# A two-layer diffusion trunk step on one core: x rebuilt upon an event, modulation sums issued with a margin, the first piece of W1 split into ring slots

## The chip, the cores and the metric

One core of one Trainium2 chip runs the whole program. The metric is the device time of one execution in microseconds, as the median of several; smaller is better. TensorE (PE) multiplies, VectorE (DVE), ScalarE (ACT) and GpSimd (POOL) do the elementwise work, SyncE (SP) issues the DMAs. Every engine works through its own instructions strictly in the order in which they were written out.

## The reference, cut to what matters

640 tokens (128 of context, 512 latent) of 1024 features go through two layers. Each layer has a mixer (layer 0: retention beside differential attention; layer 1: windowed attention beside gated linear attention, GLA) and a squared-ReLU MLP, 1024 to 4096 to 1024. Around both stands the same frame:

```python
mod = (silu(cond) @ w_mod[l] + b_mod[l])        # shift, scale, gate of mixer and of MLP
x = layer_norm(ALPHA * x + gate_a * mixer(x * (1 + scale_a) + shift_a), g_a, b_a)
h = x * (1 + scale_m) + shift_m
x = layer_norm(ALPHA * x + gate_m * (square(relu(h @ w_1)) @ w_2), g_m, b_m)
```

Everything is fp32. The latent tokens have one conditioning vector, the context tokens another.

## The kernel before

**Tiles.** The tokens are NT = 5 tiles of 128. An fp32 product is three float32r products: each operand is split into a high part (`hh`, `whi`, `ghi`) and the rest (`hl`, `wlo`, `glo`), and PE adds high by high, high by low and low by high. In the MLP the hidden features come in 8 groups `g` of 512. For each group, W1 is applied with the weights stationary (matmuls `ff`, 96 per token half), ReLU is squared and split (`relu`, `ghi`, `glo`), and W2 is applied (`fps`, 120 matmuls of 512 columns). In group 0 the first 256 tokens go ahead of the other 384 (`ff1`), since the tiles of the norm ahead become ready one by one; in the trace these are `ff` matmuls of 256 and of 384 columns.

**Weights.** A `Unit` (L507 to L531) is 512 KB of weights. It is loaded into one of three buffers `wraw` and split: ACT copies the high part (`whi`), DVE subtracts (`wlo`), both into rings of NSPL = 5 buffers. `background` (L674) splits ahead of need, by at most five units; while the out projection of the second half holds four, one unit of W1 can be split ahead. A pool of 44 slots of 128x512 fp32, the ring (`slot(...)`), holds nearly everything else, x among it.

**Order.** The program is written out by a planner. It simulates the engines on a clock of its own and decides for each engine which instruction is written next. PE's main work is a list, worked off in order (`order.gemm(step)`). All else are chains: Python generators that are spawned and go on as their turn comes. A chain that yields a number is resumed that many planner microseconds later; one that yields a function, when the function is true; one that yields nothing, when its last instructions are over. On the chip no such wait exists. What the planner leaves is the place of each instruction in its engine's queue, and semaphores for the data alone.

**Modulation.** A `ModChunk` computes 512 columns of `mod` for both conditions in 8 steps (`step`, one per 128 rows of w_mod): POOL multiplies the loaded rows (`wmod`) and adds them up (`moda`), and for the other condition DVE does both in one instruction (layer 1's columns) or ACT and POOL share it (layer 0's). After the eighth step `finish` (L586) issues four small matmuls (`modps`, 256 columns) on PE that add over the partitions. Eight chunks are done in layer 0's mixer, twelve (all of layer 1's) in layer 0's MLP.

**Norm.** `norm` (L859 on) runs once per tile: DVE takes the statistics, POOL writes x <- x * r + nmr in place, PE transposes it (`lnT`), ACT applies scale and shift (`h`) and copies the high part (`hh`), DVE subtracts (`hl`). What the matmuls after it need is complete with `hl`. The residual x still has to be multiplied by the norm's gain and get its bias added: `update` does so on POOL, four instructions of 128x512 per tile (x with `lnrow`), 20 per norm. I call this the rebuild. It is spawned with a delay of UPD = (40, 30) planner microseconds, 40 behind the norm ahead of the MLP (the attention norm), 30 behind the norm after it (the MLP norm). In layer 0 the MLP norm's rebuilt x is written to DRAM and read again by the out projection of layer 1.

**Lines of the profile.** All instructions of DVE, ACT and POOL are recorded at L377, DMAs at L451, matmuls at L467 and transposes at L477; they are told apart by the names of their tiles. In the changed kernel these numbers are one lower, as a constant goes.

Of the kernel before, what the change touches and what calls it, by code (L numbers as in the profile page):

```python
# [9 lines left out]
F32 = mybir.dt.float32  # L10
F32R = mybir.dt.float32r
# [26 lines left out]
LO_POOL = 0  # L38
UPD = (40.0, 30.0)
DRS = False  # L40
# [364 lines left out]
def trunk_kernel(ctx: ExitStack, tc: tile.TileContext, io: dict, layers: int = 2, stop: str = ""):  # L405
# [101 lines left out]
    class Unit:  # L507


        def __init__(self, src, kt, n):  # L510
            self.src, self.kt, self.n = src, kt, n

# [6 lines left out]
        def split(self):  # L519
            tot = self.kt * self.n  # L520
            raw, self.raw = self.raw, None
            hi = wspl.tile([P, UW], F32R, tag="whi", name=nm("whi"))
            lo = wspl.tile([P, UW], F32R, tag="wlo", name=nm("wlo"))
            order.reuse("whi", NSPL, hi)
            order.reuse("wlo", NSPL, lo)
            act.copy(hi[:, :tot], raw[:, :tot])
            vec_tt(lo[:, :tot], raw[:, :tot], hi[:, :tot].bitcast(F32), op=ALU.subtract)
            self.time = order.step[-1]
            self.hi = hi[:, :tot].rearrange("p (k n) -> p k n", k=self.kt)
            self.lo = lo[:, :tot].rearrange("p (k n) -> p k n", k=self.kt)  # L530

    class Piece:


        def __init__(self, units):
            self.units = units
            self.where = [(u, k) for u in units for k in range(u.kt)]

        def hi(self, k, s=slice(None)):
            u, j = self.where[k]  # L540
            return u.hi[:, j, s]

        def lo(self, k, s=slice(None)):
            u, j = self.where[k]
            return u.lo[:, j, s]

    mods, cols = {}, {}

    class ModChunk:
# [36 lines left out]
        def finish(self):  # L586

            l, a = self.l, self.c % 2
            kind = self.c // 2
            if a == 0:  # L590
                mods[l, kind] = dram.tile([2, 2, 512], F32, name=nm("mrow"))
# [37 lines left out]
    for l in range(layers):  # L629
# [8 lines left out]
        for g in range(8):  # L638
            for n in range(2):
                add_piece((l, "1", 2 * g + n), [Unit(io["w_1"][l, 2 * g + n, u], 4, 256) for u in range(2)])  # L640
            for n in range(2):
                add_piece((l, "2", g, n), [Unit(io["w_2"][l, g, n, u], 2, 512) for u in range(2)])
# [31 lines left out]
    def background():  # L674

        saved = order.step
        if pos[0] < min(pos[1] + NSPL, pos[2]) and order.over(units[pos[0]].there):
            split_unit()
# [179 lines left out]

    def norm(t, rows, ft, A, B, final, key, xd=None):  # L859

# [28 lines left out]
        if final:  # L889
# [13 lines left out]
            return  # L903
        def update():
            for a in range(2):
                x = xn[a][:, :512]
# [13 lines left out]
        for a in range(2):  # L920
# [8 lines left out]
            (pool if a < LO_POOL and t < NT - 1 else dve).tensor_tensor(ft.l[a][:, :, tcol(t)], h4, hi.bitcast(F32), op=ALU.subtract)  # L929
        order.spawn(update(), UPD[xd is not None])  # L930
        yield
# [548 lines left out]
    def odd_mixer(ft, cat, out_half):  # L1480
# [343 lines left out]
        value_project((1, "GV0"), ft, G[0].vs)  # L1824
        order.spawn(gla_chain(0))
        sq(0)
        later(lambda: swa(0), 3.5)
# [36 lines left out]
    def layer(l, ft, xd):  # L1864
# [26 lines left out]
        for t in range(NT):  # L1891
            for a in range(2):
                order.gemm(lambda: out_projection(l, cat, env, 1, t, a), cond)
            order.spawn(norm(t, ln, ft, A, B, False, ("m", l, t)))
        del cat, env
# [3 lines left out]
        for g in range(8):  # L1899
            last = g == 7  # L1900
            parts = [(slot("ghi")[:, :TOK].bitcast(F32R), slot("glo")[:, :TOK].bitcast(F32R)) for _ in range(4)]
            if g == 0:
# [47 lines left out]
            else:  # L1950
# [8 lines left out]
                for t in range(NT):  # L1959
                    for nh in range(2):  # L1960
                        order.gemm(lambda: mlp_block(t, nh))
                    order.spawn(norm(t, ln, ft_n, A, B, last_layer, ("h", l, t), xd[t]))
        if last_layer:
# [116 lines left out]
```

## Time and profile before

| | |
|---|---|
| three runs, median | 1718.78 us (1714.31, 1718.78, 1721.03) |
| profiled execution, its own time | 1719.93 us |
| span of that execution in the trace | 1718.1 us |
| PE busy | 1592.2 us, 93% |
| PE weight load (PEld) busy | 1437.5 us, 84% |
| DVE busy | 1096.0 us, 64% |
| POOL busy | 727.4 us, 42% |
| ACT busy | 649.8 us, 38% |
| mean granted TensorE clock | 0.965 |

The span is the time from the first to the last recorded instruction. Layer 0's mixer reaches to about 385 us, its out projection and MLP to about 912 us, layer 1's mixer to about 1170 us and the last MLP to the end. Busy times are unions over an engine's instructions. The granted clock is that of TensorE as the profile's rows show it: 1.00 stands for 2.4 GHz and 0.50 for 1.2 GHz. In a row of the timeline the bracket at the end says how long the engine had been idle before it and whose instruction ended that.

### The profile page before, as it was taken

Reading aid. Unit: us, or ns where it says so; the run is one execution under the profiler, and the core shown is the slowest. Engines: PE = TensorE matmul, PEld = TensorE weight load, DVE = VectorE, ACT = ScalarE, POOL = GpSimd, SP = SyncE. Lnnn points to the kernel's source line nnn. Section 1 sums busy time; section 2 is a strip of 40 time slices with the busy share of each in tenths; the row PEclk is TensorE's granted clock in tenths of the full one; section 3 lists DMA queues with packets and bytes.
Section 4 is the critical chain, followed back from the end, with each engine's and each line's share of the span. In section 5 each row is a group of like instructions: output and inputs, shape, how many; then the busy total and the mean of one; then the engine's idle time right before and its main releaser. Section 6 shows DMA issues by size and latency. Waiting matters only on the chain.

```text
span 1718.1 us, 27804 instructions
## 1 busy us (share of the span) xinstructions
PE 1592.2 (93%) x10869; PEld 1437.5 (84%) x10869; DVE 1096.0 (64%) x1953; ACT 649.8 (38%) x1338; POOL 727.4 (42%) x625
## 2 busy tenths in 40 slices
PE   7888989989888999999899999979989999999995
PEld 4887888889777998898688988869979889988994
DVE  2787875588656666776757678777862444434458
ACT  2564554344431322232126645554443223222221
POOL 1786666671595556555705535431170000000115
PEclk9998999999899999999999999989989999999998
DMA  9432333452245545445232311113212222223221
GB/s 336 155 95 88 108 94 105 126 171 72 69 126 147 142 139 162 137 143 166 86 93 81 114 51 46 30 53 114 75 63 85 74 74 74 74 74 99 74 74 61
DMA packets 89522, 178.22 MB, mean 104 GB/s; under 512 B 23360, under 2 KB 30512, under 8 KB 89392
## 3 DMA queue, kind: packets, MB, share of 16 engines
q1 hardware_dynamic: 89392, 176.46, 32.8%
q8 instruction: 85, 1.39, 0.3%
q14 instruction: 45, 0.37, 0.1%
HBM read 169.92 MB, written 6.50 MB: 103 GB/s over the span
## 4 chain that ended last, share of the span: by engine, by line
PE 70%; DVE 14%; POOL 7%; ACT 4%; issue 3%; DMA 2%; SPq 0%; POOLq 0%; ACTq 0%; DVEq 0%
PE ff L467 24%; PE fps L467 22%; PE proj L467 8%; PE ops L467 4%; POOL moda L377 3%; PE fproj L467 2%; DMA wmod<-in_w_mod 2%; POOL wmod L377 2%; DVE wlo L377 2%; PE early L467 1%; PE po L467 1%; DVE hl L377 1%; POOL x L377 1%; DVE x L377 1%; PE gl L467 1%
## 5 line engine op out<-in xcount | busy, mean ns | idle before, releaser
L467 PE MATMUL ff<-hl,whi 128*128 128x320 f32 (+2 forms) x1024 | 319.8, 312 | 8.8 <-DVE hl L377 8.8
L467 PE MATMUL ff<-hh,whi 128*128 128x320 f32 (+2 forms) x1024 | 321.0, 313 | 4.5 <-ACT hh L377 4.5
L467 PE MATMUL ff<-hh,wlo 128*128 128x320 f32 (+2 forms) x1024 | 319.7, 312 | 3.2 <-DVE wlo L377 3.2
L377 ACT CAST whi<-wraw 128x1024 fp32r<-128x1024 f32 (+1 forms) x187 | 193.8, 1043 | 284.2 <-PE fps L467 220.2
L377 DVE TENSOR_TENSOR wlo<-wraw,whi 128x1024 fp32r<-128x1024 f32 (+1 forms) x187 | 250.3, 1343 | 63.6 <-ACT whi L377 63.3
L467 PE MATMUL fps<-wlo,ghi 128*128 128x512 f32 (+1 forms) x648 | 254.2, 392 | 2.0 <-DVE wlo L377 2.0
L467 PE MATMUL fps<-whi,ghi 128*128 128x512 f32 (+1 forms) x648 | 255.0, 394 | 0.0
L467 PE MATMUL fps<-whi,glo 128*128 128x512 f32 (+1 forms) x648 | 253.9, 392 | 0.0
L377 POOL TENSOR_SCALAR wmod<-wmod,cs 128x512 f32<-128x512 f32 x140 | 141.2, 1009 | 155.3 <-DVE moda L377 132.9
L377 POOL TENSOR_TENSOR moda<-moda,wmod 128x512 f32<-128x512 f32 x140 | 201.6, 1440 | 9.1
L467 PEld LDWEIGHTS ff<-hl,whi 128*128 128x128 f32 x1024 | 195.4, 191 | 10.0 <-DVE hl L377 9.4
L467 PEld LDWEIGHTS ff<-hh,whi 128*128 128x128 f32 x1024 | 195.4, 191 | 8.9 <-ACT hh L377 5.0
L467 PEld LDWEIGHTS ff<-hh,wlo 128*128 128x128 f32 x1024 | 195.3, 191 | 4.0 <-DVE wlo L377 4.0
L377 DVE TENSOR_TENSOR relu<-relu 128x320 f32<-128x320 f32 (+3 forms) x100 | 66.6, 666 | 198.0 <-ACT ghi L377 197.5
L377 POOL TENSOR_TENSOR y<-y,gate 128x512 f32<-128x512 f32 x20 | 33.1, 1659 | 357.2 <-DVE y L377 355.7
L377 ACT ACTIVATE relu<-ff 128x320 f32<-128x320 f32 (+3 forms) x100 | 51.3, 513 | 319.1 <-PE ff L467 319.1
L377 DVE TENSOR_TENSOR y<-fps,y 128x512 f32<-128x512 f32 x120 | 82.5, 689 | 118.1 <-PE fps L467 118.1
L467 PEld LDWEIGHTS fps<-wlo,ghi 128*128 128x128 f32 x648 | 122.0, 188 | 30.2 <-DVE wlo L377 3.3
L467 PEld LDWEIGHTS fps<-whi,ghi 128*128 128x128 f32 x648 | 122.1, 188 | 29.3 <-issue 2.0
L467 PEld LDWEIGHTS fps<-whi,glo 128*128 128x128 f32 x648 | 122.0, 188 | 28.2
L377 POOL TENSOR_TENSOR x<-x,lnrow 128x512 f32<-128x512 f32 (+1 forms) x76 | 113.3, 1510 | 47.0 <-ACT x L377 45.5
L377 POOL TENSOR_TENSOR moda<-moda,modp 128x512 f32<-128x512 f32 x56 | 82.0, 1465 | 88.7 <-ACT modp L377 88.4
(285 smaller groups left out, 3553.9 us busy)
## 6 DMA issues: line engine op xcount, KB each, us to landing
wraw<-in_w SPq DMA_DIRECT2D x128, 512.0 KB
wmod<-in_w_mod SPq DMA_DIRECT2D x192, 256.0 KB
wraw<-in_w_even SPq DMA_DIRECT2D x24, 512.0 KB
wraw<-in_w_out SPq DMA_DIRECT2D x16, 512.0 KB
wraw<-in_w_odd SPq DMA_DIRECT2D x16, 512.0 KB
gate<-mrow SPq DMA_DIRECT2D x16, 256.0 KB
xT<-in_xT SPq DMA_DIRECT2D x8, 320.0 KB
brow<-in_b_mod SPq DMA_DIRECT2D x40, 64.0 KB
```

The source lines that it names most:

```text
L377: i = f(*a, **k)
L467: nc.tensor.matmul(o, a, b, **kw)
```

## The change

It has three parts, in the words of the code:

1. The rebuild no longer starts after a fixed delay. `update` starts with `yield when`: behind the attention norm it waits until group 1 of the MLP begins to be written out, behind layer 0's MLP norm until the projection `sq(0)` of layer 1's mixer does. UPD goes.
2. `finish` starts with `yield 10.0`: the four `modps` matmuls of a chunk are issued 10 planner microseconds later than before.
3. The first piece of W1 of each layer (two units, `own=True`) isn't split into the rings of five but into slots of the 44-slot ring, in pieces of 128x512: per unit two casts on ACT and two subtractions on DVE in place of one each. These units don't count toward the five, so `background` may split them earlier.

```diff
-UPD = (40.0, 30.0)
...
+            if self.own:
+
+                self.hs, self.ls = [], []
+                for k in range(0, self.kt, 2):
+                    c = slice(k * self.n, min(k + 2, self.kt) * self.n)
+                    w = c.stop - c.start
+                    h, l_ = slot("whs")[:, :w].bitcast(F32R), slot("wls")[:, :w].bitcast(F32R)
+                    act.copy(h, raw[:, c])
+                    vec_tt(l_, raw[:, c], h.bitcast(F32), op=ALU.subtract)
...
+            yield 10.0
             if a == 0:
                 mods[l, kind] = dram.tile([2, 2, 512], F32, name=nm("mrow"))
             ps = acc("modps")
...
-                add_piece((l, "1", 2 * g + n), [Unit(io["w_1"][l, 2 * g + n, u], 4, 256) for u in range(2)])
+                add_piece((l, "1", 2 * g + n), [Unit(io["w_1"][l, 2 * g + n, u], 4, 256, g + n == 0) for u in range(2)])
...
-        if pos[0] < min(pos[1] + NSPL, pos[2]) and order.over(units[pos[0]].there):
+        held = sum(not u.own for u in units[pos[1]:pos[0]])
+        if pos[0] < pos[2] and (units[pos[0]].own or held < NSPL) and order.over(units[pos[0]].there):
             split_unit()
...
         def update():
+            yield when
             for a in range(2):
...
-        order.spawn(update(), UPD[xd is not None])
+        order.spawn(update())
...
+        done.add(("SQ", 0))
         sq(0)
...
-            order.spawn(norm(t, ln, ft, A, B, False, ("m", l, t)))
+            order.spawn(norm(t, ln, ft, A, B, False, ("m", l, t), when=lambda: ("g", l, 1) in done))
...
+            if g > 0:
+                done.add(("g", l, g))
...
-                    order.spawn(norm(t, ln, ft_n, A, B, last_layer, ("h", l, t), xd[t]))
+                    order.spawn(norm(t, ln, ft_n, A, B, last_layer, ("h", l, t), xd[t], lambda: ("SQ", 0) in done))
```

Since the planner simulates all engines together, the order of much else shifts as well. The counts hardly do: PE has 9294 rows before and after, ACT 1138 and 1150, DVE 1882 and 1877, POOL 630 and 630.

**POOL at the start of layer 0's MLP.** The first two rows are the last tile's x of the attention norm; rows with `lnrow` are the rebuild; `wmod` and `moda` are the first chunk of layer 1's modulation (`cs` holds the conditions). Before:

```order
L377 TENSOR_SCALAR x_4425<-x_4425,r_5180,nmr_5186 128x512
L377 TENSOR_SCALAR x_4630<-x_4630,r_5180,nmr_5186 128x512
L377 TENSOR_TENSOR x_4259<-x_4259,lnrow_4660 128x512
L377 TENSOR_TENSOR x_4259<-x_4259,lnrow_4664 128x512
L377 TENSOR_TENSOR x_4465<-x_4465,lnrow_4662 128x512
L377 TENSOR_TENSOR x_4465<-x_4465,lnrow_4666 128x512
L377 TENSOR_TENSOR x_4313<-x_4313,lnrow_4660 128x512
L377 TENSOR_TENSOR x_4313<-x_4313,lnrow_4664 128x512
L377 TENSOR_SCALAR moda_5475<-wmod_4455,cs 128x512
L377 TENSOR_SCALAR wmod_4548<-wmod_4548,cs 128x512
L377 TENSOR_TENSOR x_4499<-x_4499,lnrow_4662 128x512
L377 TENSOR_TENSOR moda_5475<-moda_5475,wmod_4548 128x512
```

Now, with five further pairs of `wmod` and `moda` left out between the two pieces:

```order
L376 TENSOR_SCALAR x_4425<-x_4425,r_5166,nmr_5172 128x512
L376 TENSOR_SCALAR x_4617<-x_4617,r_5166,nmr_5172 128x512
L376 TENSOR_SCALAR moda_5489<-wmod_4455,cs 128x512
L376 TENSOR_SCALAR wmod_4499<-wmod_4499,cs 128x512
L376 TENSOR_TENSOR moda_5489<-moda_5489,wmod_4499 128x512
...
L376 TENSOR_SCALAR wmod_5588<-wmod_5588,cs 128x512
L376 TENSOR_TENSOR moda_5489<-moda_5489,wmod_5588 128x512
L376 TENSOR_SCALAR moda_5693<-wmod_5627,cs 128x512
L376 TENSOR_TENSOR x_4134<-x_4134,lnrow_4647 128x512
L376 TENSOR_TENSOR x_4313<-x_4313,lnrow_4647 128x512
L376 TENSOR_TENSOR x_4134<-x_4134,lnrow_4651 128x512
```

The whole first chunk now stands ahead of the rebuild, and all 20 instructions of the rebuild stand within the second chunk (`moda_5693`). Before, six stood ahead of the first chunk and 14 within it. In layer 1's MLP there is no modulation, and POOL's order there is what it was: ten x with r and nmr, then the 20 of the rebuild.

**PE at the second chunk's sums.** `hh`, `hl`, `whi`, `wlo` belong to W1 of group 1, `ghi`, `glo` with `fps` to W2. Before, the four matmuls stand in group 1 of layer 0's MLP, 24 `ff` matmuls ahead of the end of its W1:

```order
L467 MATMUL ff_5970<-hl_4677,whi_5760 128x320
L467 MATMUL ff_5970<-hh_4675,wlo_5761 128x320
L467 MATMUL modps_6000<-moda_5688,ones 32x256
L467 MATMUL modps_6000<-moda_5689,ones 32x256
L467 MATMUL modps_6000<-moda_5688,ones 32x256
L467 MATMUL modps_6000<-moda_5689,ones 32x256
L467 MATMUL ff_6018<-hh_4674,whi_5659 128x320
```

Now they stand behind 108 of the 120 `fps` of the same group:

```order
L466 MATMUL fps_6215<-whi_6060,ghi_5716 128x512
L466 MATMUL fps_6215<-wlo_6061,ghi_5716 128x512
L466 MATMUL fps_6215<-whi_6060,glo_5717 128x512
L466 MATMUL modps_6229<-moda_5692,ones 32x256
L466 MATMUL modps_6229<-moda_5693,ones 32x256
L466 MATMUL modps_6229<-moda_5692,ones 32x256
L466 MATMUL modps_6229<-moda_5693,ones 32x256
L466 MATMUL fps_6244<-whi_5967,ghi_5710 128x512
```

That is 132 matmuls later (24 `ff`, 108 `fps`). The first chunk's sums stand 24 `ff` later than before, the twelfth's 108 matmuls later.

**POOL from layer 0 to layer 1.** Around the rebuild stand the first instructions of GLA's first head group: `gA` is set to zero, `Eq` and `Ek` are computed level by level (128x5x64 is the first level). Before, the last rows of the rebuild and what follows:

```order
L377 TENSOR_TENSOR x_4598<-x_4598,lnrow_9152 128x512
L377 MEMSET gA_10013 128x5
L377 MEMSET gA_10021 128x5
L377 TENSOR_TENSOR x_4598<-x_4598,lnrow_9156 128x512
L377 TENSOR_TENSOR x_4425<-x_4425,lnrow_9150 128x512
L377 TENSOR_TENSOR x_4425<-x_4425,lnrow_9154 128x512
L377 TENSOR_TENSOR x_4630<-x_4630,lnrow_9152 128x512
L377 TENSOR_TENSOR x_4630<-x_4630,lnrow_9156 128x512
L377 TENSOR_TENSOR Eq_10184<-gA_10021 128x5x64
L377 TENSOR_TENSOR Eq_10184<-gA_10013 128x5x64
L377 TENSOR_TENSOR Ek_10185<-gA_10013 128x5x64
```

Now, from the last x with r and nmr on, with seven rows of the rebuild left out:

```order
L376 TENSOR_SCALAR x_4617<-x_4617,r_9584,nmr_9590 128x512
L376 MEMSET gA_10001 128x5
L376 MEMSET gA_10009 128x5
L376 TENSOR_TENSOR x_4134<-x_4134,lnrow_9158 128x512
...
L376 TENSOR_TENSOR x_4425<-x_4425,lnrow_9158 128x512
L376 TENSOR_TENSOR Eq_10172<-gA_10009 128x5x64
L376 TENSOR_TENSOR x_4425<-x_4425,lnrow_9162 128x512
L376 TENSOR_TENSOR Eq_10172<-gA_10001 128x5x64
L376 TENSOR_TENSOR Ek_10173<-gA_10001 128x5x64
L376 TENSOR_TENSOR Ek_10173<-gA_10009 128x5x64
L376 TENSOR_TENSOR x_4465<-x_4465,lnrow_9160 128x512
```

Nine rows of the rebuild stay ahead of GLA's first level; one stands within it and ten between it and the second level.

On DVE, between the attention norm's last `nmr` and its last `hl`, that one counted, stood 9 instructions in either layer; now 14 do. The changed order has three `wlo` there in place of one, as W1's second piece can be split there too.

In both mixers the last transposes of the heads' outputs (`catT`), which the out projection of the second half h=1 needs, have moved within the 240 `ops` matmuls of the first half h=0: in layer 0 from behind 192 of them to behind all 240, in layer 1 from behind 96 to behind 216.

## Rows read from the trace of the kernel before

**Rows 1.** The page: span, and each engine's busy time with its share.

```profile
span 1718.1 us, 27804 instructions
...
PE 1592.2 (93%) x10869; PEld 1437.5 (84%) x10869; DVE 1096.0 (64%) x1953; ACT 649.8 (38%) x1338; POOL 727.4 (42%) x625
```

**Rows 2.** Windows (columns in the first line): layer 0's mixer, layer 1's mixer, last MLP.

```profile
core 0: us, PE busy (x) PEld busy (x) DVE busy (x) ACT busy (x) POOL busy (x), PEclk, DMA share, GB/s
70.00:385.00 315.00, 280.11 (x2179) 263.27 (x2177) 232.62 (x531) 160.44 (x387) 215.41 (x174) 0.95 0.37 111
...
912.00:1170.00 258.00, 238.92 (x2376) 215.42 (x2376) 193.74 (x457) 143.01 (x372) 121.75 (x134) 0.96 0.20 65
...
1278.00:1670.00 392.00, 392.00 (x2183) 354.39 (x2182) 165.40 (x212) 108.02 (x151) 17.43 (x11) 1.00 0.25 81
```

**Rows 3.** PE's waits: us in total, times, longest.

```profile
PE modps L467 <- POOL moda L377: 13.1, 4, 4.6
PE ff L467 <- DVE hl L377: 8.8, 2, 4.5
...
PE ff L467 <- ACT hh L377: 4.5, 2, 2.2
...
PE modps L467 <- DVE moda L377: 3.6, 2, 2.1
...
PE ff L467 <- DVE wlo L377: 3.2, 4, 1.0
```

**Rows 4.** Timeline of PE, layer 0's MLP: start us, us, instruction, [idle before <-releaser].

```profile
499.53 0.71 PE L467 MATMUL modps<-moda,ones 128*32 128x256 f32 x6 [4.64 <-POOL moda L377]
...
525.36 1.08 PE L467 MATMUL modps<-moda,ones 128*32 128x256 f32 x6 [3.86 <-POOL moda L377]
...
851.30 1.08 PE L467 MATMUL modps<-moda,ones 128*32 128x256 f32 x6 [4.32 <-POOL moda L377]
```

**Rows 5.** Windows as in rows 2: what follows three of these waits, and `ff`'s wait for `hl` in layer 0.

```profile
499.94:503.36 3.42, 3.42 (x16) 3.19 (x13) 0.45 (x2) 0.00 (x0) 3.42 (x5) 0.50 0.85 281
525.36:530.67 5.31, 5.31 (x22) 4.50 (x23) 1.98 (x4) 0.00 (x0) 2.58 (x3) 0.50 0.46 121
...
851.30:854.93 3.63, 3.63 (x12) 2.34 (x13) 2.44 (x4) 0.00 (x0) 2.42 (x2) 0.50 0.13 52
...
440.10:445.33 5.23, 5.23 (x16) 5.23 (x17) 0.54 (x1) 0.00 (x0) 1.02 (x1) 0.50 0.00 0
```

**Rows 6.** Timeline of DVE: start of layer 0's MLP.

```profile
425.50 0.42 DVE L377 TENSOR_TENSOR relu<-relu 128x256 f32<-128x256 f32 x1
...
431.08 1.40 DVE L377 TENSOR_TENSOR relu<-relu 128x256 f32<-128x256 f32 x1
```

**Rows 7.** Timeline of POOL: layer 0's MLP, its end, layer 1's MLP.

```profile
429.95 9.54 POOL L377 TENSOR_TENSOR x<-x,lnrow 128x512 f32<-128x512 f32 x6
...
461.45 0.94 POOL L377 TENSOR_SCALAR wmod<-wmod,cs 128x512 f32<-128x512 f32 x1 [20.33 <-DVE moda L377]
...
928.93 23.36 POOL L377 TENSOR_TENSOR x<-x,lnrow 128x512 f32<-128x512 f32 x15
...
1248.69 30.18 POOL L377 TENSOR_TENSOR x<-x,lnrow 128x512 f32<-128x512 f32 x20
```

**Rows 8.** The page's costliest groups (line, engine, instruction, count | busy us, mean ns | idle before).

```profile
L377 POOL TENSOR_SCALAR wmod<-wmod,cs 128x512 f32<-128x512 f32 x140 | 141.2, 1009 | 155.3 <-DVE moda L377 132.9
L377 POOL TENSOR_TENSOR moda<-moda,wmod 128x512 f32<-128x512 f32 x140 | 201.6, 1440 | 9.1
```

**Rows 9.** Chain that ended last, layer 1's out projection and last MLP: start us, us, what.

```profile
1186.86 19.97 PE ops L467 x168
...
1278.38 28.02 PE fps L467 x120
1306.40 28.16 PE ff L467 x192
```

**Rows 10.** Timeline of DVE behind layer 1's last transposes.

```profile
1188.81 1.55 DVE L377 TENSOR_TENSOR catl<-soT,cath 128x640 fp32r<-128x640 f32 x2
```

More of the change, by code (lines that the diff above doesn't have):

```diff
@@ L507, in trunk_kernel, with __init__ @@
     class Unit:
-        def __init__(self, src, kt, n):
-            self.src, self.kt, self.n = src, kt, n
+        def __init__(self, src, kt, n, own=False):
+            self.src, self.kt, self.n, self.own = src, kt, n, own
         def load(self):
@@ L521, in split @@
             raw, self.raw = self.raw, None
+            if self.own:
[6 more added lines that the diff above has]
+                    vec_tt(l_, raw[:, c], h.bitcast(F32), op=ALU.subtract)
+                    self.hs.append(h)
+                    self.ls.append(l_)
+                self.time = order.step[-1]
+                return
             hi = wspl.tile([P, UW], F32R, tag="whi", name=nm("whi"))
@@ L537, in __init__, with part @@
             self.where = [(u, k) for u in units for k in range(u.kt)]
+        @staticmethod
+        def part(u, tiles, j, s):
+            return tiles[j // 2].rearrange("p (k n) -> p k n", n=u.n)[:, j % 2, s]
         def hi(self, k, s=slice(None)):
             u, j = self.where[k]
-            return u.hi[:, j, s]
+            return self.part(u, u.hs, j, s) if u.own else u.hi[:, j, s]
         def lo(self, k, s=slice(None)):
             u, j = self.where[k]
-            return u.lo[:, j, s]
+            return self.part(u, u.ls, j, s) if u.own else u.lo[:, j, s]
     mods, cols = {}, {}
@@ L857, in summed, with norm @@
             stt(x, x, ALPHA, y, op0=ALU.mult, op1=ALU.add)
-    def norm(t, rows, ft, A, B, final, key, xd=None):
+    def norm(t, rows, ft, A, B, final, key, xd=None, when=None):
         cuts = [(0, 0, 512), (1, 0, 512)] if t < NT - 1 else [(0, 0, 256), (0, 256, 512), (1, 0, 256), (1, 256, 512)]
```

## The prediction

> **What bounds the kernel now.** I read the page first: PE is busy for 93% of the span [rows 1], and a span of 1718.1 less 1592.2 us of work leaves 126 us in which it does nothing. So a change that adds or takes no matmul can win only out of these 126 us, or out of stretches in which PE works at a lower clock. Next, the windows, to see where the 126 us lie. The last MLP has none of them: 392.00 busy of 392.00 us at a granted clock of 1.00 [rows 2]. Layer 0's mixer has 34.9 (315.00 less 280.11), layer 1's 19.1 (258.00 less 238.92) [rows 2]. Then the list of PE's waits, for what the change can reach: the sums `modps` wait 13.1 us for POOL's `moda` and 3.6 for DVE's; at the starts of the two MLPs `ff` waits 8.8 us for `hl`, 4.5 for `hh`, 3.2 for `wlo` [rows 3]. That is 33 us in all. Last, windows behind such waits: the granted clock stands at 0.50 for some us, though PE has work without a gap [rows 5]. A wait costs more than its own length here.
>
> **Modulation sums with a margin.** This removes waits and adds none by itself. All of DVE's 3.6 us and 12.8 of POOL's 13.1 (4.64, 3.86 and 4.32, the three long ones [rows 4]) fall on the first, second and twelfth chunk in layer 0's MLP, where PE otherwise has no cause to stop: 16.4 us. Behind the three waits PE works 3.42, 5.31 and 3.63 us at 0.50 [rows 5]; at 1.00 these take half, so 6.2 us more are at stake. Together 22.6 us. Do the sums now come late enough? An `ff` matmul takes 28.16 / 192 = 0.147 us and an `fps` 28.02 / 120 = 0.233 [rows 9].
>
> - First chunk: the sums move by 24 `ff`, 3.5 us. That is less than the wait of 4.64, but POOL's chain for the chunk loses 14 instructions of the rebuild. A rebuild's instruction takes 30.18 / 20 = 1.51 us [rows 7], so it loses 21 us and ends long before.
> - Second chunk: the sums move by 24 `ff` and 108 `fps`, 3.5 + 25.2 = 28.7 us. But the whole rebuild, 30.2 us, now stands inside this chunk's chain, with seven times `wmod` and `moda` at 1.009 + 1.440 [rows 8], 17.1 us, so the chain is 47.3 us long. It begins when the first chunk's ends. If that chunk's `wmod` is released at 461.45 as before [rows 7], the first chunk ends near 479 and the second near 526. PE gets there near 525.36 − 3.86 − 1.4 − 4.64 − 1.7 − 6 + 28.7 = 536 (its old time, less the two waits ahead of these sums, the earlier wait with its slow stretch and the next paragraph's gain, plus the shift). The margin is 10 us; it is the smallest.
> - Twelfth chunk: 108 matmuls later, at least 15.9 us, against waits of 4.32 and 2.1.
>
> I take −22. Ends: −14 if the second chunk's sums still wait by half of what they did and the clock falls once more, −23 if all goes. The `modps` themselves and the DMA of their result move along; the next reader of layer 1's columns is its own mixer, hundreds of us later.
>
> **Rebuild behind layer 0's attention norm.** Six instructions of it run at 429.95, for 9.54 us [rows 7], just while DVE prepares the last operands of the MLP. A `relu` of 256 columns takes 0.42 us at 425.50 and 1.40 at 431.08 [rows 6]: beside the rebuild each DVE instruction takes about 1 us longer. Of the waits at MLP starts, 16.5 us in two layers [rows 3], layer 0 has 8.1: one of each of the two pairs for `hh` and `hl` (2.2 and 4.3) and half of the four for `wlo`. The 5.23 us of work at 0.50 behind the last one [rows 5] cost another 2.6. Of these 10.7 us I expect 6 back. With the rebuild moved behind the first chunk DVE works at the short durations; but 14 instead of 9 instructions now stand ahead of the last `hl`, and ACT's part of the chain (`h`, `hh`), which POOL does not slow, then ends last. Ends: −3.5 (only the two `hl` and `wlo` parts shrink), −8.5.
>
> **Rebuild behind layer 1's attention norm.** By the order nothing moves: the planner's event has no other POOL work to let pass, so the 20 instructions follow the last `nmr` as before and run for 30.18 us from 1248.69 [rows 7]. DVE goes on being slowed there, and has five more instructions. At 1.40 us each [rows 6] these would put `hl` 7 us later, but they start some 3 us earlier, as the `wlo` in front of them have gone into ring slots earlier, and 1 us of wait for `wlo` goes. I take 0, between −3 and +5.
>
> Here a rule stands against the change. Rows 6 show DVE slowed to about the pace of one of POOL's instructions, 1.40 against 1.51 us, not stopped for longer. The Trainium skill, in "SBUF — State Buffer", section "SBUF: two separate sides", says that the port pair of VectorE and GpSimd is an exclusive lock, which an instruction holds until its end, while the other fully blocks. The rows agree for the small `relu`. By that rule each of the five added instructions could wait for a whole one of POOL's, 5 × 1.51 = 7.6 us, and with no earlier start the sum would be some 7 us higher; that is a rival below.
>
> **Rebuild from layer 0 to layer 1.** Fifteen of its instructions ran from 928.93 for 23.36 us [rows 7] beside the last `hl`. Nine still do; the other eleven, 17 us, now stand in and behind the first GLA level. For DVE at this place: 0. The x that goes through DRAM lands later by about 20 us, which the out projection, more than 100 us on, doesn't notice. For GLA see the next part.
>
> **The mixers' order.** That is the cost that the trace of before doesn't show. The last transposes now come behind 240 instead of 192 of layer 0's h=0 matmuls, and 216 instead of 96 in layer 1. What stands between them and h=1 covers the way from transpose to `catl`: 19.97 / 168 = 0.119 us per matmul [rows 9], so 5.7 us of cover become none, and 17.1 become 2.9. The way itself is a copy, a cast and the subtraction, of which two take 1.55 us [rows 10]; I put it at 3 to 5 us. So +2.5 to 3 in layer 0 and +2 to 2.5 in layer 1. In return, later transposes may wait less for the heads. Sum: +5; ends −8 (a quarter of the mixers' 54 us of idle time goes, less the cover lost) and +18 (GLA in layer 1 late by most of 17 us and half of layer 0's way in front).
>
> **Split of the own units.** Four casts and four subtractions of 512 columns in place of two and two of 1024: the same columns, on engines that are far from full, earlier than the stretch that matters. 0.
>
> Sum: −22 − 6 + 0 + 0 + 5 + 0 = −23 against 1719.93 us, the profiled execution's own time: 1697. The median of the runs shown is 1718.78, 1.1 lower; I leave the sum as it is.
>
> **Rivals.**
>
> - *Sums that still wait.* The second chunk has a margin of 10 us out of estimates; if DMA or DVE hold up the first chunk, the rebuild's 30 us in the chain eat it. For it: POOL's wait of 20.33 us for DVE ahead of the first chunk [rows 7]. Against it: all other chunks have no rebuild any more. Price: half of the 22 and the 6 kept back, so about 1707 us.
> - *The mixers gain as well.* The planner fitted all of it anew; were 20% to 30% of the 54 us idle in mixers to go, about 1683. Against it: nothing in the change aims there.
> - *The mixers eat the savings.* The covers of 5.7 and 17.1 us are lost, and heads end no earlier: +17 more, about 1714, within the noise.
> - *Slower: GLA's chain gets too late.* Eleven instructions of the rebuild, 17 us, stand on POOL ahead of the second level's `Eq` and `Ek`. If POOL, not PE, sets the pace of the levels, the last transposes of layer 1 come 17 us later, without the 14 us of cover, and the half clock behind such a wait adds some 5. 1719.93 − 28 for the two gains + 36 for this is 1728, and 1733 with the start of layer 1's MLP 5 us worse. It decides once these losses exceed the gains by the measurement's bound, some 37 us in all. Against it: POOL is 42% busy [rows 1] and 122 of 258 us in this mixer [rows 2], so it can catch up.
> - *Each added DVE instruction in layer 1 waits for a whole one of the rebuild*, 5 × 1.51 us, and none starts earlier: about 1704. For it: 1.40 against 0.42 us [rows 6]. Against it: the added `wlo` find their operands ready earlier.
>
> **How the numbers follow.** Forecast (1688 to 1706) 0.43; added DVE instructions blocked 0.05; sums that still wait 0.19; mixers gain 0.10; mixers eat it 0.14; slower 0.09. I predict 1697 us. The range is 1681 to 1716: it leaves out the slower rival and the edges. A measurement can tell about 0.5% from no change here, 8.6 us. Forecast, blocked DVE, waiting sums and mixers' gain are faster by more than that, 0.77, of which I take off 0.02 as 1707 lies close to the bound: faster 0.75, same 0.16, slower 0.09.
>
> **What would show it.** In the profile of the changed kernel: no `modps` row with a bracket above 1 us in layer 0's MLP, and no window at 0.50 behind one; PE busy nearly all of 500 to 850. At the start of layer 0's MLP the `relu` at 0.4 and not 1.4 us and the wait for `hl` at 2 us or less; in layer 1 still 20 x with `lnrow` in one run beside a `hl` wait of about 4.5 us. Ahead of h=1, new waits for `catl` of 2 to 3 us in both layers. The prediction is wrong if the waits for `moda` stay, or if the mixers (70 to 385 and 912 to 1170) get longer by more than 10 us together.

## The result, and the profile after

The changed kernel takes 1705.82 us, the median of 8 runs (1699.45 to 1711.06), against 1717.43 us before (8 runs, 1714.31 to 1721.03). The ratio is 0.9933, with a 95% interval of 0.9917 to 0.9949: faster by 0.67%, or 11.6 us. The forecast was 1697, with a range of 1681 to 1716. The profiled execution took 1705.05 us with a span of 1702.9, so it stands 15.2 us under the span of before [rows 1], 3.6 us more than the medians differ by.

I cut both spans at the same places of the program: the first `ff` and the first `fps` of each layer, and layer 1's first `proj`. Windows of the kernel before; columns as in rows 2. From top to bottom: layer 0's mixer with the out projection, the start of its MLP, the rest of its MLP, layer 1's mixer with the out projection, the start of its MLP, the rest.

```profile
0.10:417.40 417.30, 364.67 (x2819) 333.49 (x2819) 288.03 (x645) 193.94 (x457) 249.53 (x213) 0.94 0.43 136
417.40:459.30 41.90, 33.78 (x211) 32.73 (x210) 26.42 (x48) 22.09 (x50) 14.75 (x11) 0.88 0.16 51
459.30:916.40 457.10, 439.68 (x2438) 386.79 (x2436) 307.44 (x366) 127.59 (x191) 259.74 (x209) 0.98 0.44 131
916.40:1236.10 319.70, 299.50 (x2885) 273.82 (x2883) 240.32 (x560) 166.75 (x423) 131.26 (x142) 0.97 0.23 72
1236.10:1278.20 42.10, 33.77 (x211) 32.87 (x210) 31.08 (x48) 22.11 (x50) 32.71 (x24) 0.88 0.15 50
1278.20:1718.10 439.90, 420.78 (x2317) 377.83 (x2316) 202.66 (x290) 117.33 (x167) 39.38 (x27) 0.98 0.24 78
```

The same six windows of the changed kernel:

```profile
0.10:416.30 416.20, 362.56 (x2818) 332.30 (x2819) 289.61 (x653) 193.82 (x459) 249.33 (x213) 0.95 0.43 139
416.30:450.50 34.20, 31.50 (x212) 30.14 (x211) 20.13 (x44) 22.07 (x52) 6.55 (x5) 1.00 0.19 63
450.50:887.10 436.60, 432.31 (x2438) 381.75 (x2436) 309.27 (x366) 126.66 (x190) 280.06 (x215) 1.00 0.44 134
887.10:1223.10 336.00, 303.49 (x2885) 277.04 (x2884) 244.06 (x567) 167.10 (x426) 130.95 (x142) 0.95 0.23 72
1223.10:1263.50 40.40, 33.42 (x212) 32.00 (x211) 35.11 (x44) 22.01 (x52) 36.09 (x24) 0.92 0.17 53
1263.50:1702.90 439.40, 420.24 (x2317) 377.80 (x2315) 199.81 (x288) 116.41 (x166) 39.53 (x27) 0.98 0.23 76
```

The first number behind the window is its length. The six differences are −1.1, −7.7, −20.5, **+16.3**, −1.7 and −0.5 us. They add up to −15.2. So the change won 31 us and lost 16, and the loss sits in one place: layer 1's mixer. There PE is idle for 32.5 us in place of 20.2, and its work takes 303.5 in place of 299.5 us, since more of it runs at the lower clock (mean 0.95 in place of 0.97).

PE's waits in the changed kernel (us in total, times, longest), the lines that answer to rows 3 and the new ones of some size:

```profile
PE ff L466 <- DVE hl L376: 6.8, 6, 4.6
...
PE sqT L476 <- DVE ropea L376: 6.4, 2, 5.9
...
PE ops L466 <- DVE tmp L376: 4.0, 1, 4.0
PE ops L466 <- ACT pT L376: 4.0, 1, 4.0
...
PE fps L466 <- DVE glo L376: 3.3, 1, 3.3
```

The sums' 16.7 us in rows 3 are gone; no `modps` stands in the list any more. `ff` still waits once for 4.6 us for `hl`, now in layer 1 alone. New are the wait of the query transposes `sqT` for `ropea` (the rotary embedding of the windowed attention's queries), two waits of `ops` in the mixers, and one of `fps` for `glo`.

How the second chunk's sums went. POOL's timeline of the changed kernel: the first `wmod` that had to wait for DVE, the end of the first chunk, the rebuild inside the second chunk, and the end of this chunk:

```profile
452.65 0.93 POOL L376 TENSOR_SCALAR wmod<-wmod,cs 128x512 f32<-128x512 f32 x1 [25.45 <-DVE moda L376]
...
472.65 1.30 POOL L376 TENSOR_TENSOR moda<-moda,wmod 128x512 f32<-128x512 f32 x1
...
474.59 15.17 POOL L376 TENSOR_TENSOR x<-x,lnrow 128x512 f32<-128x512 f32 x9
...
493.47 15.42 POOL L376 TENSOR_TENSOR x<-x,lnrow 128x512 f32<-128x512 f32 x9
...
525.46 1.30 POOL L376 TENSOR_TENSOR moda<-moda,wmod 128x512 f32<-128x512 f32 x1
```

And PE's, at the sums that need it:

```profile
535.85 0.64 PE L466 MATMUL modps<-moda,ones 128*32 128x256 f32 x8
```

POOL ends at 526.8 us and PE comes at 535.9: a margin of 9 us, where the prediction had 526 and 536. There is no bracket on PE's row, so it waited for nothing. That POOL's end came out to the microsecond is partly luck: its chain was released at 452.65, 8.8 us before the 461.45 that the prediction took over from before, but the first chunk took 21.3 us in place of 17.5 and the second 52.8 in place of 47.3.

### The profile page after: what moved, and what is told of

Its sections match the earlier page's. It is cut to its first block, busy times and chain, and to the rows that moved or that the text cites. A ratio compares the mean times of both kernels' runs of the same rounds, so it can differ in the third digit from the quotient of the medians.

```text
span 1702.9 us, 27816 instructions
## 1 busy us (share of the span) xinstructions
PE 1583.5 (93%) x10869; PEld 1431.0 (84%) x10869; DVE 1098.0 (64%) x1957; ACT 648.1 (38%) x1342; POOL 742.5 (44%) x625
## 5 line engine op out<-in xcount | busy, mean ns | idle before, releaser
L466 PE MATMUL ff<-hh,whi 128*128 128x320 f32 (+2 forms) x960 | 297.0, 309 | 0.0
L466 PE MATMUL ff<-hh,wlo 128*128 128x320 f32 (+2 forms) x960 | 296.2, 308 | 0.0
L466 PE MATMUL ff<-hl,whi 128*128 128x320 f32 (+2 forms) x960 | 296.1, 308 | 0.0
L376 DVE TENSOR_TENSOR wlo<-wraw,whi 128x1024 fp32r<-128x1024 f32 (+1 forms) x183 | 245.8, 1348 | 76.3 <-ACT whi L376 76.1
L376 ACT CAST whi<-wraw 128x1024 fp32r<-128x1024 f32 (+1 forms) x183 | 189.4, 1045 | 251.7 <-PE fps L466 230.3
L376 POOL TENSOR_TENSOR moda<-moda,wmod 128x512 f32<-128x512 f32 x140 | 206.9, 1478 | 9.4
L376 DVE TENSOR_TENSOR relu<-relu 128x320 f32<-128x320 f32 (+3 forms) x100 | 74.3, 743 | 179.6 <-ACT ghi L376 178.7
L466 PEld LDWEIGHTS ff<-hh,whi 128*128 128x128 f32 x960 | 180.2, 188 | 3.4 <-issue 2.5
L466 PEld LDWEIGHTS ff<-hl,whi 128*128 128x128 f32 x960 | 180.2, 188 | 0.6
L466 PEld LDWEIGHTS ff<-hh,wlo 128*128 128x128 f32 x960 | 180.2, 188 | 0.0
```

Source lines behind the costliest of these rows:

```text
L376: i = f(*a, **k)
L466: nc.tensor.matmul(o, a, b, **kw)
```

## The experiments

Line numbers in the excerpts are those of the profile of each kernel; they differ by one or two. "Middle" is the third window above, "start" the second or the fifth, "mixer" the fourth.

**1. The later sums alone** (the kernel before with one line more).

```diff
             kind = self.c // 2
+            yield 10.0
```

> The kernel before with one line of the change alone: the modulation sums issued 10 planner microseconds later. If the sums' waits are what the middle of layer 0's MLP gained (457.1 us from its first W2 matmul to layer 1's first projection before, 436.6 after), this stretch alone falls to 437 +-2 us here too, with no modps wait above 1 us. Layer 1's mixer stays at about 320 us if the rebuild's event made it 336 long; the total would then be some 19 to 23 us under the kernel before, about 1696, and so under the changed kernel. Rival: any shift of the planner's order costs layer 1's mixer some 16 us, whatever caused it; then the total is 1700 to 1705 and this mixer takes about 335 us.

Measured: 1701.64 us, ratio 0.9919 (0.9900 to 0.9937). The mixer takes 319.3 us, as in the theory, and the middle 443.0, not 437. No `modps` waits, but `fps` now waits 6.55 us for `glo` in group 1. The rival has the total (1700 to 1705) and not its cause, as the mixer didn't grow to 335. So this one line is worth as much as the whole change, and it doesn't cost the mixer anything.

**2. The events alone**, without the later sums and without the slots.

```diff
-            yield 10.0
...
-[Unit(io["w_1"][l, 2 * g + n, u], 4, 256, g + n == 0) for u in range(2)]
+[Unit(io["w_1"][l, 2 * g + n, u], 4, 256 ) for u in range(2)]
```

> The rebuild upon an event alone, without the later sums and without W1's split into slots. If the event makes layer 1's mixer longer, it takes about 336 us here (320 before), layer 0's MLP start takes about 36 to 38 us in place of 41.9, and the middle of layer 0's MLP stays near 455 or loses some of its waits, since the chunk's chain on POOL is free of the rebuild for the first chunk: total 1722 to 1732, slower than before. Rival, that the mixer's loss comes from the other two parts: mixer at 320, total 1708 to 1714.

Measured: 1730.07 us, ratio 1.0079 (1.0064 to 1.0094), slower than before. Mixer 339.5, first start 36.6, middle 454.6: as the theory had it. In the middle the waits of the sums are replaced by one of 9.65 us of `fps` for ACT's `ghi`; run 10 shows where that comes from.

**3. The changed kernel with a narrow rebuild behind layer 0's MLP norm.** The planner sees the full instructions, the chip gets 16 of 512 columns, so x is rebuilt there only in part; every engine's order is the same.

```diff
-                pool.tensor_tensor(x, x, rows[0][a][:, :512], op=ALU.mult)
+                pool.tensor_tensor(x, x, rows[0][a][:, :512], op=ALU.mult, narrow=16 if key[0] == "h" else 0)
```

> The changed kernel with every engine's order as it is, but the 20 instructions of the rebuild behind layer 0's MLP norm are 16 columns wide in place of 512, so x is rebuilt there only in part: the rest keeps its place, and POOL no longer reads and writes beside DVE from 943 to 957 us. Theory: the contention of the moved rebuild with DVE makes the 5.89 us wait of the transposes of the windowed attention's queries for ropea and the 13.65 us at half clock behind it; then the wait is under 2 us, the clock does not fall there, and layer 1's mixer takes 321 to 326 us in place of 336: total 1693 to 1696. Rival: the new place of ropea on DVE, behind the first GLA level, makes the wait; then it stays above 4 us, the mixer at 332 to 336, and the total at 1702 to 1706.

Measured: 1703.91 us (0.9925, 0.9906 to 0.9944), mixer 336.3. The theory falls. PE's wait and DVE's row ahead of it in the changed kernel:

```profile
968.48 0.66 PE L476 MATMUL sqT<-cst,qq 128*128 128x128 f32 x2 [5.89 <-DVE ropea L376]
```

```profile
962.23 2.00 DVE L376 COPY gST<-gl 64x320 f32<-64x320 f32 x4 [1.41 <-PE gl L466]
```

Timelines of this run's kernel, PE first:

```profile
965.63 0.66 PE L478 MATMUL sqT<-cst,qq 128*128 128x128 f32 x2 [5.89 <-DVE ropea L378]
```

```profile
953.08 0.82 DVE L378 TENSOR_TENSOR Ek<-Ek,gkT 128x640 f32<-128x640 f32 x1
959.38 2.00 DVE L378 COPY gST<-gl 64x320 f32<-64x320 f32 x4 [5.48 <-PE gl L468]
961.39 3.27 DVE L378 TENSOR_TENSOR_SCAN gA<-ones,ge 128x128 f32<-128x128 f32 x10
964.67 0.82 DVE L378 TENSOR_TENSOR ropea<-proj,cst 128x256 f32<-128x256 f32 x3
```

The wait is 5.89 us, to the hundredth the same as in the changed kernel, though DVE was early here: it stood idle for 5.48 us, in place of 1.41, waiting for PE's `gl` (the scores of the first GLA level). Behind that wait, on DVE's queue, stand the copy of `gl`, ten scans and then `ropea`, 2.00 + 3.27 + 0.82 us. PE's queue has `sqT` right behind `gl`. So PE runs `gl` and then waits for the whole row behind it, however fast anyone was before. Two queues that fit together badly make this wait, not contention.

**4. The changed kernel with a narrow rebuild behind layer 1's attention norm**, likewise (`narrow=16 if key[:2] == ("m", 1) else 0`), so x is rebuilt only in part there.

> The changed kernel with every engine's order as it is, but the 20 instructions of the rebuild behind layer 1's attention norm are 16 columns wide, so x is rebuilt there only in part. Theory: the 4.59 us wait of ff for hl and the half clock behind it (6.83 us) come from the rebuild that runs beside DVE; then the wait falls below 1.5 us, the clock stays at 1.00, and the time from the first ff to the first W2 matmul falls from 40.4 to 34 us, as in layer 0 (34.2): total 6 us less than the changed kernel, about 1700. Rival: the 14 instructions ahead of the last hl are too many for DVE in any case; then it stays at 39 to 40 and the total at 1705.

Measured: 1696.26 us (0.9886, 0.9862 to 0.9910). The window of layer 1's MLP start:

```profile
1218.30:1252.40 34.10, 31.45 (x210) 30.14 (x209) 20.09 (x43) 21.92 (x52) 12.80 (x24) 1.00 0.20 62
```

34.1 us at a clock of 1.00, against 40.4 at 0.92. What is left of layer 1's wait for `hl` is the rebuild beside DVE, and nothing else.

**5. The event behind layer 0's MLP norm taken back**, the old delay of 30 put in its place; all else as in the changed kernel.

```diff
-            yield when
+            yield when if xd is None else 30.0
```

> The changed kernel, with the rebuild behind layer 0's MLP norm put back to its delay of 30 planner microseconds; the event behind the attention norm, the later sums and the slots stay. Theory: that one event moves the first GLA level 72 matmuls later on PE, right ahead of the transposes of all five tiles' queries, and this order costs layer 1's mixer its 16 us. Then the mixer falls from 336 to 318 to 324 us with all else as in the changed kernel, and the total is about 1690. Rival: the sums' 10 us or the slots shift the mixer's order just as much: mixer 330 or more, total 1700 or more.

Measured: 1690.86 us (0.9846, 0.9823 to 0.9869), mixer 322.1 us. The window of the mixer:

```profile
885.60:1207.70 322.10, 297.10 (x2886) 271.83 (x2884) 244.77 (x567) 167.16 (x425) 133.27 (x142) 0.97 0.23 75
```

The theory stands for the event: taking it out of the changed kernel gives the mixer 14 us back. PE's order in this kernel has its transposes of the queries spread among the projections again.

**6. The event set one projection later**, ahead of `sq(1)`.

```diff
-        done.add(("SQ", 0))
         sq(0)
...
+        done.add(("SQ", 0))
         sq(1)
```

> The changed kernel with the event of the rebuild behind layer 0's MLP norm set one projection later: ahead of sq(1) in place of sq(0). The first GLA level then stands on PE where it stood before the change. Theory (the late first level is what costs): mixer 318 to 325 us, total 1688 to 1695. Rival (a rebuild anywhere inside the mixer costs, for DVE or for the planner): mixer 330 to 340 us, total 1700 to 1708, with new waits behind sq(1).

Measured: 1715.59 us (0.9991, 0.9979 to 1.0002), mixer 350.1. The theory that only the late first level costs falls: this order has the first level in its old place and loses 14 us more, beyond the rival's 340 too. POOL, ACT and PE in this kernel:

```profile
1029.24 12.06 POOL L376 TENSOR_TENSOR x<-x,lnrow 128x512 f32<-128x512 f32 x9
1041.26 1.25 POOL L376 TENSOR_TENSOR gqb<-gA 128x640 f32<-128x640 f32 x1
```

```profile
1042.55 0.74 ACT L376 ACTIVATE gqb<-gqb 128x640 f32<-128x640 f32 x1 [16.13 <-POOL gqb L376]
...
1050.49 0.74 ACT L376 ACTIVATE Eq<-Eq 128x640 f32<-128x640 f32 x1 [4.04 <-POOL Eq L376]
1051.13 0.58 ACT L376 COPY sqT<-sqT 128x128 f32<-128x128 f32 x3
```

```profile
1051.43 1.12 PE L476 MATMUL spT<-cst,sp 128*128 128x128 f32 x4 [15.05 <-ACT sqT L376]
```

Nine instructions of the rebuild stand ahead of `gqb` on POOL. ACT waits 16.13 us for `gqb` and, further on, 4.04 us for `Eq`, both from POOL; copies of `sqT`, which need nothing from POOL, are queued behind both; PE waits 15.05 us, until one of these copies is done at 1051.4.

**7. The same with a narrow rebuild behind the MLP norm**, every engine's order as in run 6, x again rebuilt only in part there.

> The kernel with the event at sq(1), every engine's order as it is, but the 20 instructions of the rebuild behind layer 0's MLP norm 16 columns wide, so x is rebuilt there only in part. Theory: nine of them, 12 us, stand on POOL ahead of gqb; ACT waits for gqb 16.13 us with a copy of sqT queued behind it, and PE waits 15.05 us for that. Then that wait falls to 3 us or less, the stretch at half clock around it goes, and layer 1's mixer falls from 350 to 322 to 332 us; total 1688 to 1698. Rival: as in the changed kernel, the order alone costs, and narrow instructions change nothing: mixer 345 to 350, total 1712 to 1716.

Measured: 1699.43 us (0.9891, 0.9875 to 0.9908), mixer 333.6; the same wait on PE and ACT's wait now:

```profile
1041.76 1.11 PE L478 MATMUL spT<-cst,sp 128*128 128x128 f32 x4 [6.21 <-ACT sqT L378]
```

```profile
1033.91 0.74 ACT L378 ACTIVATE gqb<-gqb 128x640 f32<-128x640 f32 x1 [3.50 <-POOL gqb L378]
```

Both readings were half right. Of the 30 us that this mixer loses against before, 16.5 are the rebuild's time on POOL and some 14 are order that stays bad when the rebuild costs nothing.

**8. The rebuild waits on the chip.** Run 5, and ahead of the first tile's rebuild POOL reads one column of the last `hl`.

```diff
+            if key[0] == "m" and t == 0:
+                pool.tensor_scalar(sm("seen", [P, 1]), ft.l[1][:, 0, TOK - 1:TOK].bitcast(F32), cs[:, 0, 0:1], 0.0, op0=ALU.mult, op1=ALU.add)
```

> As the run with the old delay, and one instruction more per attention norm: POOL reads one column of the last hl ahead of the first tile's rebuild, so that the rebuild waits on the chip, not only in the planner, for DVE's last operand of the MLP. Theory: in layer 1 nothing else held the rebuild back from DVE; with the wait the time from the first ff to the first W2 matmul falls from 40 to about 34 to 35 us, with no wait for hl above 1.5 us and no half clock there; total 6 us under the run with the old delay, about 1684. Rival: the rebuild then slows DVE in the rest of group 0 and PE waits for glo in place of hl: the same 40 us and no gain in total.

Measured: **1684.62 us, ratio 0.9814 (0.9793 to 0.9835)**, the shortest median here. POOL in layer 1:

```profile
1233.07 0.30 POOL L376 TENSOR_SCALAR seen<-hl,cs 128x1 f32<-128x1 f32 x1 [9.83 <-DVE hl L376]
1233.33 29.84 POOL L376 TENSOR_TENSOR x<-x,lnrow 128x512 f32<-128x512 f32 x20
```

The start of layer 1's MLP takes 34.2 us. The 30 us of rebuild run beside the `ff` matmuls of the later half, and PE doesn't wait for `glo` in layer 1, so the rival falls.

**9. Later sums and slots, no event.**

```diff
-            yield when
...
-        order.spawn(update())
+        order.spawn(update(), UPD[xd is not None])
```

> The later sums and W1's first piece in slots, without either event. Against the run with the later sums alone (1701.6 us) this shows what the slots bring by themselves. Theory: little; the start of layer 0's MLP stays at 41 us as the rebuild still runs beside the last hl, only the two waits for wlo (0.97 and 0.6 us) may go, mixers as in that run: total 1699 to 1703. Rival: the slots, not the event, shortened the start of layer 0's MLP: 34 to 37 us there, total 1693 to 1697.

Measured: 1697.87 us (0.9886, 0.9867 to 0.9906). The starts take 37.6 and 40.3 us (41.2 and 42.1 in run 1), the middle 443.9, the mixer 319.7. The theory is off: the slots alone shorten both starts, by 3.6 and 1.8 us. The rival has the first start nearly right and the total not.

**10. Run 8 without the slots.**

```diff
-[Unit(io["w_1"][l, 2 * g + n, u], 4, 256, g + n == 0) for u in range(2)]
+[Unit(io["w_1"][l, 2 * g + n, u], 4, 256 ) for u in range(2)]
```

> The kernel whose rebuild waits on the chip for the last hl (1684.6 us), without the slots for W1's first piece. If the slots bring something by themselves (1701.6 against 1697.9 us in the two runs without the events), the starts of the two MLPs take 35 to 37 us in place of 34.1, with waits for wlo of 1 and 0.6 us and for hh of 2.2 us again: total 1687 to 1691. Rival: with the rebuild gone from DVE they bring nothing: starts at 34, total 1684 to 1686.

Measured: 1702.54 us (0.9915, 0.9900 to 0.9929). Both starts take 36.8 us, as expected, some 2.7 more each. But the total is 18 us over run 8, half of it in the middle (448.6 against 439.2). ACT and PE there:

```profile
508.33 1.05 ACT L376 CAST whi<-wraw 128x1024 fp32r<-128x1024 f32 x1 [0.70 <-PE ff L466]
527.56 0.72 ACT L376 ACTIVATE moda<-wmod,cs 128x512 f32<-128x512 f32 x1 [18.18 <-DMA wmod<-in_w_mod]
528.19 0.42 ACT L376 ACTIVATE relu<-ff 128x320 f32<-128x320 f32 x1
528.64 0.47 ACT L376 ACTIVATE ghi<-relu 128x320 fp32r<-128x320 f32 x1
```

```profile
529.16 0.79 PE L466 MATMUL fps<-whi,ghi 128*128 128x512 f32 x1 [10.89 <-ACT ghi L376]
```

ACT's first instruction of a modulation chunk waits 18.18 us for its rows of w_mod, with `relu` and `ghi` of the MLP queued behind it. Run 2 has the same on ACT, with 16.63 us. But the late load is not what sets run 10 apart from run 8, where ACT waits about as long for it:

```profile
508.16 0.47 ACT L376 ACTIVATE ghi<-relu 128x320 fp32r<-128x320 f32 x1
...
526.44 0.73 ACT L376 ACTIVATE moda<-wmod,cs 128x512 f32<-128x512 f32 x1 [15.93 <-DMA wmod<-in_w_mod]
```

There `relu` and `ghi` stand ahead of the waiting instruction, in run 10 behind it: the order decides. That the load is late because the rebuild holds POOL, and with it the buffers of w_mod, fits all three runs; it was not tried by itself.

**11 and 12. Run 8 with the event at group 2, and (likewise, with a 4) at group 4.**

```diff
-when=lambda: ("g", l, 1) in done
+when=lambda: ("g", l, 2) in done
```

> The kernel whose rebuild waits on the chip for the last hl, with its event one group later, at group 2 of the MLP. Theory: the 3.3 us wait of fps for glo in group 1 of layer 0 (and 6.8 us at half clock behind it) comes from the rebuild beside DVE in that group; in a later group PE meets it with more ahead, or it moves along to group 2. If it goes: middle of layer 0's MLP 433 us in place of 439, total 1679; if it moves along, 437 to 440 and 1684.

> The same with the event at group 4. Expected as for group 2: 1679 if the wait for glo belongs to group 1 alone, 1684 if the rebuild slows DVE before an fps in any group; x must be ready for group 6 (ALPHA x enters there), which leaves two groups, some 110 us, for 30 us of work, so no loss from that.

Measured: 1687.95 us (0.9834, 0.9814 to 0.9854) and 1696.22 us (0.9877, 0.9862 to 0.9892). The wait of `fps` for `glo` moves along with the rebuild and grows: 3.31 us in group 1, 4.59 in group 2, 8.62 and 3.20 in group 4. Both totals are above the two that were expected (1679 or 1684). Group 4 is worse than group 1; groups 1 and 2 are not told apart, as the intervals overlap. Why the wait grows was not looked into.

## Why the prediction was right, and where it was not

The time lies in the range, and most terms came near their size; the term for the mixers did not. The prediction called itself wrong if the two mixers together got longer by more than 10 us. With their out projections they got longer by 15.2, so by its own sign its account of the mixers is wrong. That the time still fell just inside the 1688 to 1706 of the forecast's case is luck. It is close to the 1707 of the rival whose sums still wait, but those waits didn't come; the loss is of the size of the rival whose mixers eat the savings (+17), from another cause.

**Modulation sums: right for the whole change, not for the later sums alone.** Expected −22, measured −20.5 in the middle. The waits and the half clock behind them went. But the later sums by themselves bring 14.2 there (run 1), and the event behind the attention norm another 5.7 (443.9 in run 9, 438.3 in run 5, which differ in this event alone). What is missing is the new wait of 3.3 us for `glo` in group 1, which the prediction didn't have: there the rebuild now stands beside DVE. In run 1 the rebuild is over by 497 us and `fps` waits 6.55 us for `glo` at 520 all the same, so the rebuild isn't all of the cause; DVE's modulation and `wlo` stand there too. (In POOL's order before, twelve of the rebuild's instructions stand within the first chunk and two within the second, not fourteen within the first; that makes the first chunk's gain smaller than assumed and changes nothing else.)

**Layer 0's MLP start: right.** Expected −6, measured −7.7. `relu` of 256 columns takes 0.43 us again and `hl` 0.69. But two causes were taken for one: the events without the slots give 36.6 us (run 2), the slots without the events 37.6 (run 9), both 34.2.

**Layer 1's MLP start: right.** Expected 0, measured −1.7, which is what the slots bring in run 9 (−1.8). An event in the planner held nothing back on the chip, as POOL had nothing else to do there. Run 4 puts the price of that at 6.3 us, and run 8 gets it back. The rival that the five added instructions would cost 7 us didn't come: each was slowed, as the last section shows, but they started earlier: the last `nmr` ends 6.2 us behind the first `ff`, in place of 10.5.

**Split of the own units: the step "0" failed.** It looked at the cost of the casts and found none; the gain is that W1's second piece can be split ahead, so that PE no longer waits for `wlo` and `hh`. It brings 2.7 and 2.6 us at the two starts (run 10), and in that order more in the middle.

**Layer 0's mixer: the cost didn't come.** Expected +2.5 to 3; measured −1.1 here. In the eleven other profiles of kernels with the later sums this stretch takes 411.1 to 417.0 us, against 417.4 before and 415.3 in run 2. Runs 3 and 4, whose instructions up to there are those of the changed kernel, take 411.5 and 411.9 where it takes 416.3, so the scatter of this stretch is larger than the term; a loss is in none of them. The transposes moved as foreseen, but no wait for `catl` of 2 to 3 us stands ahead of h=1, in either layer. Layer 0 in the changed kernel, the last 24 matmuls of h=0, the last transposes, and their `catl`:

```profile
377.17 0.58 PE L466 MATMUL ops<-whi,cath 128*128 128x256 f32 x1 [4.00 <-DVE tmp L376]
...
382.26 0.71 PE L476 MATMUL catT<-cst,o 128*128 128x128 f32 x5
```

```profile
383.58 0.89 DVE L376 TENSOR_TENSOR catl<-catT,cath 128x512 fp32r<-128x512 f32 x2
```

The way from transpose to `catl` took 2.2 us, not 3 to 5, and the first matmuls of h=1 ran meanwhile, so it needed no cover among those of h=0. The wait of 4.0 us for `tmp` is another one, ahead of the end of h=0; before, `catT` waited 3.44 us near there, at 376.01.

**Layer 1's mixer: the term that failed.** The prediction put it at +2 to 2.5, for lost cover ahead of h=1; it is +16.3. The end of +18 for both mixers holds it, by luck: the mechanism named for that end, POOL setting the pace of GLA's levels, isn't it (run 3). The loss is in how PE's new order meets DVE's. One place shows it: `sqT` ends 5.89 us of waiting and stands in a stretch of low clock,

```profile
965.68:979.34 13.66, 9.41 (x36) 7.31 (x37) 9.66 (x34) 4.92 (x22) 3.08 (x7) 0.50 0.00 1
```

9.41 us of work that at 1.00 would take an estimated 4.7. With the wait that is 10.6 us in one place. Further on stand new waits of 3.4, 2.4 and 4.0 us, up to the out projection, while two of before, 5.7 and 3.0, are gone. Nearly all of it came with the event behind the MLP norm (without it the mixer is 2.4 us longer than before, run 5): in the planner's order nine rows of the rebuild stand ahead of the first level's `Eq`, and PE's `gl` of that level stands 72 matmuls later, right ahead of the transposes. That the one made the other is argued from the order, not shown.

So the forecast of −23 stands against −11.6 of the medians. Without that one event the same change gives 1690.86, 26.6 us under the 1717.45 of before measured beside it: near the forecast, as most other terms were.

## What to carry to other kernels

Where a planner writes a kernel's order, an event inside the planner holds back nothing on the chip; where an instruction must keep away from another engine's hot stretch, let it read what ends that stretch (0.30 us of POOL's time bought 6 us). Price a moved step also by what the planner then writes elsewhere: read both engines' new queues side by side at each place where one waits for the other, since a row such as `gl`, `sqT` on PE against `gl`'s copy, scans, `ropea` on DVE shows the wait before anything runs. And put a margin ahead of small matmuls that wait for a slow engine: one line was worth 14 us.

## What the runs showed of the hardware that was not expected

The prediction had a DVE instruction lose about 1 us beside POOL's rebuild, from one `relu`. It loses about the same time whatever its size. DVE in the changed kernel, at the start of layer 0's MLP (rebuild elsewhere) and of layer 1's (rebuild from 1232.83 on, 20 instructions in 31.70 us):

```profile
428.45 1.23 DVE L376 TENSOR_TENSOR wlo<-wraw,whi 128x1024 fp32r<-128x1024 f32 x1 [0.40 <-ACT whi L376]
429.67 0.69 DVE L376 TENSOR_TENSOR hl<-h,hh 128x512 fp32r<-128x512 f32 x1
...
433.61 0.43 DVE L376 TENSOR_TENSOR relu<-relu 128x256 f32<-128x256 f32 x1 [0.60 <-ACT ghi L376]
...
1236.18 2.31 DVE L376 TENSOR_TENSOR wlo<-wraw,whi 128x1024 fp32r<-128x1024 f32 x1
1238.42 1.77 DVE L376 TENSOR_TENSOR hl<-h,hh 128x512 fp32r<-128x512 f32 x1
...
1243.99 1.49 DVE L376 TENSOR_TENSOR relu<-relu 128x256 f32<-128x256 f32 x1
```

1024, 512 and 256 columns lose 1.08, 1.08 and 1.06 us. With the narrow rebuild of run 4 the same three instructions of layer 1 take 1.29, 0.70 and 0.43 us, so the loss is the rebuild's. A share of bandwidth would take more from the long ones; a wait for the end of one of POOL's instructions need not, and these take 31.70 / 20 = 1.58 us here. No row shows the wait itself. The Trainium skill, in "SBUF — State Buffer", section "SBUF: two separate sides", tells it as such a wait: the port pair that VectorE and GpSimd share is an exclusive lock and not a split of bandwidth. The rows of DVE agree, with about 1.07 us as the price of each encounter.
